# Two transposes of P in one run, and an opening whose loads wait for x

## The chip, the cores and the metric

The kernel runs on one core of one Trainium2 chip. The metric is the device time of one execution in microseconds, the median of several runs. TensorE (PE in the rows) multiplies, VectorE (DVE) and ScalarE (ACT) do the elementwise work, GpSimd (POOL) and SyncE (SP) mostly issue DMAs. An engine executes its instructions in the order in which the program lists them, and an instruction waits until what it reads is ready and what it overwrites is free.

## The reference

x has 256 rows of 1024 floats. Four layers, then one block of another kind:

```python
for i in range(DEPTH):                      # 4
    x = layer_norm(ALPHA * x + 0.5 * swiglu(x, ffn1_w13[i], ffn1_w2[i]), ...)
    y = (dsa_mixer, fox_mixer, mla_mixer)[i % 3](x, ...)
    x = layer_norm(ALPHA * x + y, ...)
    x = layer_norm(ALPHA * x + 0.5 * swiglu(x, ffn2_w13[i], ffn2_w2[i]), ...)

# the second block
qa, ka, va, u, qm, km, vm, gates = split_in(rms_norm_2(x) @ w_in)
ya = swa_attention(qa, ka, va, sinks, slopes) @ w_o_swa
z  = gelu(s5_ssm(u, ...)) @ w_glu
yb = (z[..., :512] * sigmoid(z[..., 512:])) @ w_o_ssm
yc = moba_attention(qm, km, vm, slopes) @ w_o_moba
g  = sigmoid(gates)
x  = x + (g[0] * ya + g[1] * yb + g[2] * yc) @ w_out
x  = x + square(relu(rms_norm_2(x) @ w_ff1)) @ w_ff2
```

All attention is softmax(q k^T + bias) v per head, with 16 heads in a layer's mixer and 8 + 8 in the second block. s5_ssm is a linear recurrence over the 256 rows with 32 groups of 64 complex states.

## The kernel before

All weights are streamed once, in tiles of 128 x 1024 floats that SyncE loads into five buffers named raw. A weight w is split: ScalarE rounds raw to `whi`, VectorE subtracts to get `wlo` (helpers at L242 and L250, eight buffers each), activations are split the same way, and a product is three matmuls: L417 (hi by hi), L418 (lo by hi) and L419 (hi by lo). TensorE's transposes are matmuls with the identity, at L449.

The program is written by Python generators ("threads"). Each emits the instructions of one piece of work, and `yield`s the time at which it may go on; `self.at["pe"]` is an estimated clock of TensorE, and whoever emits long streams of matmuls lets the threads that are due step in between. So the estimated times set the order in which an engine's instructions stand. At run time that order is fixed.

PSUM has eight banks: four named y, two acc and two tr. `can("tr", n)` gives the time at which n banks of that name are free. Every run of transposes takes a tr bank and gives it back when ScalarE or VectorE has copied it out.

Attention (`attend`) works in groups of up to eight heads, in two halves of even and odd heads: scores at L701 into two y banks, mask and minimum on VectorE at L713, exponential on ScalarE, sums and scaling on VectorE; then each half's P (a tile named wk) is transposed by up to four transposes, copied to SBUF (the first half by ScalarE, the second by VectorE in most stages), and multiplied with v at L758. Five stages do this: the mixers of the layers (DSA, FoX, MLA, DSA) and the second block's (SWA and MoBA).

In the second block the SSM runs beside attention, in four segments s, each a chain: eight matmuls at L1387 into two y banks; on VectorE eight products with tables named tb, two sums, eight scans (named wk) and six more operations; then

```python
            yield lambda: max(t, self.can("tr"))
            yb = self.bank("tr")
```

and output matmuls at L1428 (`part` None) and L1430 (parts 0 and 1, which read the chain's two results); a GELU on ScalarE, split into two tiles named g, which the matmuls with w_glu read. A segment's tables are loaded by GpSimd once the segment before has its output matmuls.

In the opening SyncE issues the first half of x's first 128 rows, the first weight tile in two halves and x's other parts in turn, while TensorE runs dummy matmuls (`warm`, L359) and then transposes x.

Of the kernel before, what the change touches and what calls it, by code (L numbers as in the profile page):

```python
# [17 lines left out]
P = 128  # L18
# [119 lines left out]
class Model:  # L138
# [179 lines left out]
    def setup(self):  # L318

        self.ident = self.load_const("ident", [P, P])  # L320
        self.mask = self.tile([P, S], "mask", 1)
        self.rope = self.const([P, NT, 2, 16], "rope")
        self.mh = self.const([P, 1], "mh")
        self.nc.vector.memset(self.mh, -0.5)
        self.nc.scalar.activation(self.small(1), self.mh, AF.Silu)
        x = [self.tile([P, 1024], f"x{T}", 1) for T in range(NT)]
        parts = [[(x[T][:, c:c + 512], self.ap["x"][T * P:(T + 1) * P, c:c + 512]) for c in (0, 512)] for T in range(NT)]
        self.between[0], self.between[0, 0], self.between[2] = [parts[0][0]], [parts[1][0]], [parts[0][1], parts[1][1]]
        self.between[10] = [(self.mask, self.ap["mask"]), (self.rope, self.ap["rope"])]
        self.skip = self.const([P, 8], "skip")  # L330
        self.sink = self.tile([P, 2, 8], "sink", 1)
        self.between[14] = [(self.skip, self.ap["ssm_d"]), (self.sink[:, 0], self.bcast(self.ap["sinks"], 8))]
        return x

    def opening(self, x):


        fut = [[Later() for _ in range(8)] for _ in range(2)]
        self.loads()
        self.pinned = True  # L340
        self.warm(7)
        th = [self.xT(x[T], T, fut[T], [self.at["pe"], 7400.0 + 700.0 * T], 1.0, False) for T in range(2)]
        for T in range(2):
            self.part_of(0, self.pieces[0].parts[T])
            next(th[T])
            ready = next(th[T])
            self.spawn(th[T], ready)
        self.pinned = False
        self.n_split = 1
        self.stream()  # L350
        return fut

# [11 lines left out]
    def take(self):  # L364
        p = self.pieces[self.taken]
        self.taken += 1
        return p

    def loads(self):

        while self.n_raw < len(self.plan) and self.n_raw < self.n_split + N_RAW:
            for out, src in self.between.get(self.n_raw, []):
                self.nc.sync.dma_start(out, src)
                self.at["dma"] += self.width(out) * 512 / 340.0
            ap = self.plan[self.n_raw]
            p = Piece()
            p.w = ap.shape[1]
            p.raw = self.tile([P, 1024], "raw", N_RAW)
            p.parts = [slice(c, c + 512) for c in (0, 512)] if self.n_raw < 2 else [slice(0, p.w)]
            for i, c in enumerate(p.parts):  # L380
                self.nc.sync.dma_start(p.raw[:, c], ap[:, c])
                if (self.n_raw, i) in self.between:
                    for out, src in self.between[self.n_raw, i]:
                        self.nc.sync.dma_start(out, src)
            t = max(self.at["dma"], self.pieces[self.n_raw - N_RAW].t if self.n_raw >= N_RAW else 0.0) + p.w * 512 / 340.0
            self.at["dma"] = t
            p.t_raw = t + 2200.0
            self.pieces.append(p)
            self.n_raw += 1
# [288 lines left out]
    def attend(self, T, n, q, k, v, bias, scale, o_tag, ot, o0, out, sink=None, gate=None, acts=False):  # L678
# [4 lines left out]
        W = P * (T + 1)  # L683
# [8 lines left out]
        def group(gi, grp):  # L692
            nc = self.nc
            yield lambda: INF if st["next"] < gi else max(inputs(grp), self.can("y", 2))
            sub = [[i for i in grp if i % 2 == e] for e in range(2)]
            banks = self.ybanks()
            for a in range(len(sub[0])):
                for t in range(T + 1):
                    for e in range(2):
                        i = sub[e][a]  # L700
                        nc.tensor.matmul(banks[e].v[:, a * W + t * P:a * W + (t + 1) * P], q(i).v, k(i, t).v, start=True, stop=True)  # L701
                        self.pe(218.0)
            t0 = self.pe_done()
            tiles, ready, PT = [], [], {}
            for e in range(2):
                yield lambda: self.load["act"] - self.busy
                ns = len(sub[e])
                sc, sm = self.wk([P, 512]), self.small(16)
                mx, ss, rc, sk = (sm[:, 4 * z:4 * z + ns] for z in range(4))
                for a, i in enumerate(sub[e]):  # L710
                    c = slice(a * W, (a + 1) * W)
                    bi, tb = bias(i)
                    nc.vector.tensor_tensor_reduce(out=sc[:, c], in0=banks[e].v[:, c], in1=bi, scale=-scale,  # L713
                                                   scalar=3.0e38, op0=OP.add, op1=OP.min, accum_out=mx[:, a:a + 1])
                    tm = self.run_on("dve", 70.0 + 1.04 * W, max(t0, tb))
                self.free(banks[e], tm)
                if sink is not None:
                    for a, i in enumerate(sub[e]):
                        self.V("tensor_tensor", mx[:, a:a + 1], mx[:, a:a + 1], sink(i)[0], op=OP.min)
                        tm = self.V("tensor_tensor", sk[:, a:a + 1], mx[:, a:a + 1], sink(i)[1], op=OP.add)  # L720
                for a, i in enumerate(sub[e]):
                    c = slice(a * W, (a + 1) * W)
                    tm = self.A(sc[:, c], sc[:, c], AF.Exp, bias=mx[:, a:a + 1], scale=-1.0, accum_out=ss[:, a:a + 1], after=tm)
                if sink is not None:
                    tm = self.A(sk, sk, AF.Exp, after=tm)
                    tm = self.V("tensor_tensor", ss, ss, sk, op=OP.add, after=tm)
                tm = self.V("reciprocal", rc, ss, after=tm)
                for a, i in enumerate(sub[e]):
                    c = slice(a * W, (a + 1) * W)
                    tm = self.V("tensor_scalar", sc[:, c], sc[:, c], rc[:, a:a + 1], None, op0=OP.mult, fast=True, after=tm)  # L730
                tiles.append(sc)
                ready.append(tm)
                if e == 0:
                    st["next"] = gi + 1
            for e in range(2):
                yield lambda e=e: max(ready[e], self.can("tr"))
                cols = len(sub[e]) * W
                b = self.transposes([tiles[e][:, j * P:(j + 1) * P] for j in range(cols // P)])
                pt = self.wk([P, 512])
                if e == 0 or acts:  # L740
                    t1 = self.A(pt[:, :cols], b.v[:, :cols], AF.Copy, after=self.pe_done())
                else:
                    t1 = self.V("tensor_copy", pt[:, :cols], b.v[:, :cols], after=self.pe_done())
                self.free(b, t1)
                for a, i in enumerate(sub[e]):
                    for t in range(T + 1):
                        PT[i, t] = pt[:, a * W + t * P:a * W + (t + 1) * P]
            yield lambda: max([t1, INF if st["pv"] < gi else 0.0] + [v(i, t).t for i in grp for t in range(T + 1)]
                              + [self.can(o_tag) if st["O"] is None else 0.0])
            if st["O"] is None:  # L750
                st["O"] = self.bank(o_tag)
            O = st["O"].v
            for a in range(len(sub[0])):
                for t in range(T + 1):
                    for e in range(2):
                        i = sub[e][a]
                        j = i // 2
                        nc.tensor.matmul(O[64 * e:64 * e + 64, j * P:(j + 1) * P], v(i, t).v, PT[i, t], start=t == 0, stop=t == T)  # L758
                        self.pe(self.pv)
            st["pv"] = gi + 1  # L760
            if gi == len(groups) - 1:
                m = n // 2
                hi, lo = ot
                t1 = self.split(hi[:, o0:o0 + m], lo[:, o0:o0 + m], self.tiles(O[:, :m * P]), self.pe_done())
                self.free(st["O"], t1)
                for j in range(o0, o0 + m):
                    out[j].put((hi[:, j], lo[:, j]), t1)

        for gi, grp in enumerate(groups):
            self.spawn(group(gi, grp), lambda: 0.0)  # L770
# [1107 lines left out]
```

## Time and profile before

| | |
|---|---|
| median of three runs | 2392.14 us (2390.95 to 2393.95) |
| the profiled execution: time, span | 2393.44 us, 2391.7 us |
| busy in the span: TensorE, VectorE, ScalarE, GpSimd | 99%, 71%, 54%, 3% |
| moved by DMA | 442.81 MB, 185 GB/s in the mean |

The span is the stretch of the profiled execution that the trace covers; the time beside it is what the device reports for that execution. A busy share is an average over the whole span.

### The profile page before, as it was taken

The numbers are of one execution on the slowest core, as the hardware profiler recorded it, in microseconds if no ns is written. First come the engines' busy times: TensorE is split into PE (matmuls) and PEld (weight loads), VectorE is DVE, ScalarE is ACT, GpSimd is POOL, SyncE is SP. The second block draws the span as 40 slices with busy tenths as digits, with TensorE's granted clock in tenths as the row PEclk, the third lists the DMA queues.
The fourth block names the chain that finished last, engine by engine and source line by source line (L and its number), as shares of the span: only waits on it lengthen the run. The fifth ranks groups of instructions, "written<-read, shape, count | busy, mean of one in ns | idle before, by whom it ended". The sixth has DMA issues, their size and how long they took to land. (4 is left out here: it accounts for less than half of the span.)

```text
span 2391.7 us, 35647 instructions
## 1 busy us (share of the span) xinstructions
PE 2369.9 (99%) x12999; PEld 1998.0 (84%) x12999; DVE 1703.6 (71%) x3265; ACT 1303.1 (54%) x2226; POOL 80.6 (3%) x123
## 2 busy tenths in 40 slices
PE   9999999999999999999999999999999999999998
PEld 7888888888888888888888888888878887878887
DVE  6668876576667866666778777666878777896664
ACT  6555655545547555455475555554665556845543
POOL 0000000000000000000000010000000000000000
PEclk9999999999999999999999999999999999999999
DMA  8655445555646465565454575654646665455552
GB/s 279 201 172 190 155 167 187 183 192 195 200 154 232 149 210 192 178 210 179 148 184 147 186 233 178 209 193 151 210 128 218 198 217 197 149 182 171 191 190 101
DMA packets 126481, 442.81 MB, mean 185 GB/s; under 512 B 14944, under 2 KB 17040, under 8 KB 126304
## 3 DMA queue, kind: packets, MB, share of 16 engines
q1 hardware_dynamic: 117792, 413.49, 51.9%
q0 software_dynamic: 7760, 26.05, 3.6%
q8 instruction: 102, 1.67, 0.3%
q10 hardware_dynamic: 752, 0.98, 0.1%
q14 instruction: 75, 0.61, 0.1%
HBM read 434.14 MB, written 5.80 MB: 184 GB/s over the span
## 5 line engine op out<-in xcount | busy, mean ns | idle before, releaser
L250 DVE TENSOR_TENSOR wlo<-raw,whi 128x1024 fp32r<-128x1024 f32 (+4 forms) x806 | 945.2, 1191 | 228.8 <-ACT whi L242 159.3
L242 ACT ACTIVATE whi<-raw 128x1024 fp32r<-128x1024 f32 (+4 forms) x806 | 821.0, 1031 | 299.9 <-PE ps L419 233.9
L426 PE MATMUL ps<-xt,whi 128*128 128x512 f32 x2496 | 628.9, 392 | 1.8 <-DVE h L250 1.4
L426 PEld LDWEIGHTS ps<-xt,whi 128*128 128x128 f32 x2496 | 451.8, 189 | 86.7 <-DVE h L250 3.8
L428 PEld LDWEIGHTS ps<-xt,wlo 128*128 128x128 f32 x2496 | 342.7, 190 | 25.8
L428 PE MATMUL ps<-xt,wlo 128*128 128x256 f32 x2496 | 350.7, 282 | 0.0
L417 PE MATMUL ps<-whi,g 128*128 128x512 f32 x866 | 339.2, 392 | 0.0
L418 PE MATMUL ps<-wlo,g 128*128 128x512 f32 x866 | 337.6, 390 | 0.0
L419 PE MATMUL ps<-whi,g 128*128 128x512 f32 x866 | 336.8, 389 | 0.0
L417 PE MATMUL ps<-whi,xt 128*128 128x512 f32 (+3 forms) x848 | 329.4, 389 | 2.6 <-DVE g L250 1.2
L419 PE MATMUL ps<-whi,xt 128*128 128x512 f32 (+3 forms) x848 | 320.5, 379 | 0.6 <-DVE xt L250 0.5
L418 PE MATMUL ps<-wlo,xt 128*128 128x512 f32 (+3 forms) x848 | 319.6, 377 | 0.0
L242 ACT ACTIVATE h<-ps 128x256 f32<-128x256 f32 x352 | 117.6, 377 | 352.5 <-PE ps L428 322.2
L250 DVE TENSOR_TENSOR h<-ps,h 128x256 f32<-128x256 f32 x320 | 122.4, 418 | 218.7 <-ACT h L242 217.9
L419 PEld LDWEIGHTS ps<-whi,g 128*128 128x128 f32 x866 | 162.7, 188 | 34.2 <-DVE g L250 0.2
L417 PEld LDWEIGHTS ps<-whi,g 128*128 128x128 f32 x866 | 162.9, 188 | 31.2
L418 PEld LDWEIGHTS ps<-wlo,g 128*128 128x128 f32 x866 | 163.0, 188 | 30.3
L417 PEld LDWEIGHTS ps<-whi,xt 128*128 128x128 f32 x848 | 159.7, 188 | 32.0 <-ACT xt L242 1.5
L419 PEld LDWEIGHTS ps<-whi,xt 128*128 128x128 f32 x848 | 159.4, 188 | 30.8 <-DVE xt L250 1.6
L418 PEld LDWEIGHTS ps<-wlo,xt 128*128 128x128 f32 x848 | 159.8, 188 | 25.7 <-issue 0.2
L242 ACT ACTIVATE g<-ps 128x512 f32<-128x512 f32 (+7 forms) x188 | 90.6, 495 | 94.9 <-PE ps L419 60.4
L242 ACT ACTIVATE h<-h 128x256 f32<-128x256 f32 x144 | 60.2, 418 | 134.7 <-DVE h L250 134.7
(222 smaller groups left out, 1924.7 us busy)
## 6 DMA issues: line engine op xcount, KB each, us to landing
raw<-in_f SPq DMA_DIRECT2D x526, 512.0 KB, 4.5
raw<-in_ff SPq DMA_DIRECT2D x64, 512.0 KB, 4.6
raw<-in_dsa_qkv SPq DMA_DIRECT2D x48, 512.0 KB, 5.1
raw<-in_w_in SPq DMA_DIRECT2D x40, 512.0 KB, 5.0
raw<-in_wo SPq DMA_DIRECT2D x32, 512.0 KB, 4.4
gb<-in_ln POOLq DMA_DIRECT2D x22, 512.0 KB, 4.7
raw<-in_fox_qk SPq DMA_DIRECT2D x16, 512.0 KB, 4.6
raw<-in_dsa_idx SPq DMA_DIRECT2D x16, 292.0 KB, 3.3
```

What stands on the lines that cost most here:

```text
L242: self.pin(self.nc.scalar.activation(out, in_, func, **kw))
L250: self.pin(getattr(self.nc.vector, fn)(out, *a, **kw))
L417: mm(acc, x[0], w[0], start=start, stop=False)
L418: mm(acc, x[0], w[1], start=False, stop=False)
L419: mm(acc, x[1], w[0], start=False, stop=stop)
L426: mm(acc, w, x.rearrange("p z t q->p (z t q)"), start=first, stop=False)
L428: mm(acc[:, S:], w, x[:, 0].rearrange("p t q->p (t q)"), start=False, stop=last)
```

## The change

In `attend`, the thread of a group waits until both halves are ready and two tr banks are free, and then emits the transposes of both halves one behind the other. In the opening, ScalarE's queue issues two of the loads (the first half of x's second 128 rows, and the second half of the first weight tile); on SyncE a one-element copy out of x's first half stands in front of the later loads, so that they wait until that half has landed; SyncE's first loads keep program order; six dummy matmuls in place of seven; and the first two weight tiles are split into hi and lo within the pinned part.

```diff
-        self.between[0], self.between[0, 0], self.between[2] = [parts[0][0]], [parts[1][0]], [parts[0][1], parts[1][1]]
+        self.between[0], self.between[2] = [parts[0][0]], [parts[0][1], parts[1][1]]
+        self.second_half = parts[1][0]
+        self.first_half = parts[0][0][0]
...
+        self.pinned = True
         self.loads()
-        self.pinned = True
-        self.warm(7)
+        self.warm(6)
...
+        for c in self.pieces[1].parts:
+            self.part_of(1, c)
         self.pinned = False
-        self.n_split = 1
+        self.n_split = 2
...
+    def sp_load(self, out, src):
+        ins = self.nc.sync.dma_start(out, src)
+        if self.n_raw < 16:
+            self.tc.keep_in_program_order(ins)
...
             for i, c in enumerate(p.parts):
-                self.nc.sync.dma_start(p.raw[:, c], ap[:, c])
-                if (self.n_raw, i) in self.between:
-                    for out, src in self.between[self.n_raw, i]:
-                        self.nc.sync.dma_start(out, src)
+                if (self.n_raw, i) == (0, 1):
+                    self.pin(self.nc.scalar.dma_start(*self.second_half))
+                    self.pin(self.nc.scalar.dma_start(p.raw[:, c], ap[:, c]))
+                    held = self.small(1)
+                    self.sp_load(held[0:1], self.first_half[0:1, 0:1])
+                else:
+                    self.sp_load(p.raw[:, c], ap[:, c])
...
-            for e in range(2):
-                yield lambda e=e: max(ready[e], self.can("tr"))
+            yield lambda: max(ready + [self.can("tr", 2)])
+            turned = [self.transposes([tiles[e][:, j * P:(j + 1) * P] for j in range(len(sub[e]) * W // P)]) for e in range(2)]
+            for e, b in enumerate(turned):
                 cols = len(sub[e]) * W
-                b = self.transposes([tiles[e][:, j * P:(j + 1) * P] for j in range(cols // P)])
                 pt = self.wk([P, 512])
```

The new lines shift the later ones by 15: L417 to L419 become L432 to L434, L449 L464, L701 L716, L758 L773, L1387 L1402, L1428 L1443 and L1430 L1445.

The instructions of two places, before and after. First the opening. SyncE's first loads before (x_6 and x_7 are the two row blocks of x, raw_76 is the first weight tile, raw_80 the second):

```order
L373 DMA x_6_71<-in_x 128x512
L381 DMA raw_76<-in_f 128x512
L384 DMA x_7_72<-in_x 128x512
L381 DMA raw_76<-in_f 128x512
L381 DMA raw_80<-in_f 128x512 x2
L373 DMA x_6_71<-in_x 128x512
L373 DMA x_7_72<-in_x 128x512
```

SyncE's first loads after (the second weight tile is raw_82):

```order
L377 DMA x_6_71<-in_x 128x512
L377 DMA raw_76<-in_f 128x512
L377 DMA small_80<-x_6_71 1x1
L377 DMA raw_82<-in_f 128x512 x2
L377 DMA x_6_71<-in_x 128x512
L377 DMA x_7_72<-in_x 128x512
L377 DMA raw_87<-in_f 128x1024
```

and ScalarE's first instructions after:

```order
L311 DMA ident_63<-in_ident 128x128
L325 ACT_TABLE_LOAD
L325 ACTIVATE small_69<-mh_67 128x1
L394 DMA x_7_72<-in_x 128x512
L395 DMA raw_76<-in_f 128x512
L242 ACTIVATE whi_102<-raw_76 128x512
L242 ACTIVATE xt_106<-ps_107 128x4x128
```

The third and fourth loads of SyncE moved to ScalarE, behind its table load and first activation, and the copy into small_80 took their place.

Second, TensorE in the second block's mixer, at the last of the SSM's four segments. Before, its eight input matmuls stand behind the last matmuls of an output projection (oth, otl), and the gates' matmuls (those that read xt) follow:

```order
L417 MATMUL ps_21312<-whi_21157,oth_4375_20026 128x512
L418 MATMUL ps_21312<-wlo_21158,oth_4375_20026 128x512
L419 MATMUL ps_21312<-whi_21157,otl_4376_20027 128x512
L1387 MATMUL ps_21413<-g_19834,pc_21377 128x128
L1387 MATMUL ps_21414<-g_19834,pc_21377 128x128
L1387 MATMUL ps_21413<-g_19834,pc_21377 128x128
L1387 MATMUL ps_21414<-g_19834,pc_21377 128x128
L1387 MATMUL ps_21413<-g_19834,pc_21377 128x128
L1387 MATMUL ps_21414<-g_19834,pc_21377 128x128
L1387 MATMUL ps_21413<-g_19834,pc_21377 128x128
L1387 MATMUL ps_21414<-g_19834,pc_21377 128x128
L417 MATMUL ps_21406<-whi_21221,xt_19766 128x512
```

After, seven of the eight stand behind the gates' matmuls, ahead of those with w_glu (that read g):

```order
L432 MATMUL ps_21512<-whi_21340,xt_19767 128x512
L433 MATMUL ps_21512<-wlo_21341,xt_19767 128x512
L434 MATMUL ps_21512<-whi_21340,xt_19767 128x512
L1402 MATMUL ps_21564<-g_19835,pc_21488 128x128
L1402 MATMUL ps_21563<-g_19835,pc_21488 128x128
L1402 MATMUL ps_21564<-g_19835,pc_21488 128x128
L1402 MATMUL ps_21563<-g_19835,pc_21488 128x128
L1402 MATMUL ps_21564<-g_19835,pc_21488 128x128
L1402 MATMUL ps_21563<-g_19835,pc_21488 128x128
L1402 MATMUL ps_21564<-g_19835,pc_21488 128x128
L432 MATMUL ps_21575<-whi_21399,g_21001 128x512
```

The eighth stands 102 rows earlier; between the two places are the gates' matmuls and the output of the segment before. The segment's output before (L1428, L1430), among the gates' matmuls:

```order
L417 MATMUL ps_21551<-whi_21321,xt_19766 128x512
L418 MATMUL ps_21551<-wlo_21322,xt_19766 128x512
L419 MATMUL ps_21551<-whi_21321,xt_19766 128x512
L1428 MATMUL ps_21564<-g_19834,rt_21379 32x128 x4
L1430 MATMUL ps_21564<-wk_21429,pc_21378 32x128 x4
L1430 MATMUL ps_21564<-wk_21431,pc_21378 32x128 x4
L1428 MATMUL ps_21564<-g_19834,rt_21379 32x128 x4
L1430 MATMUL ps_21564<-wk_21429,pc_21378 32x128 x4
L1430 MATMUL ps_21564<-wk_21431,pc_21378 32x128 x4
L417 MATMUL ps_21551<-whi_21333,xt_19766 128x512
L418 MATMUL ps_21551<-wlo_21334,xt_19766 128x512
```

and the first rows of it after, where L1443 and L1445 stand for L1428 and L1430:

```order
L434 MATMUL ps_21575<-whi_21411,g_21509 128x512
L1443 MATMUL ps_21615<-g_19835,rt_21490 32x128 x4
L432 MATMUL ps_21650<-whi_21423,g_21001 128x512
L433 MATMUL ps_21650<-wlo_21424,g_21001 128x512
L434 MATMUL ps_21650<-whi_21423,g_21002 128x512
L432 MATMUL ps_21650<-whi_21423,g_21001 128x512
L433 MATMUL ps_21650<-wlo_21424,g_21001 128x512
L434 MATMUL ps_21650<-whi_21423,g_21002 128x512
L432 MATMUL ps_21650<-whi_21438,g_21508 128x512
L433 MATMUL ps_21650<-wlo_21439,g_21508 128x512
L434 MATMUL ps_21650<-whi_21438,g_21509 128x512
L1445 MATMUL ps_21615<-wk_21582,pc_21489 32x128 x4
```

The output moved from among the gates' matmuls to the middle of the matmuls with w_glu.

## Rows read from the trace of the kernel before

**Rows 1.** The page's busy times: us, share of the span, instructions.

```profile
PE 2369.9 (99%) x12999; PEld 1998.0 (84%) x12999; DVE 1703.6 (71%) x3265; ACT 1303.1 (54%) x2226; POOL 80.6 (3%) x123
```

**Rows 2.** TensorE's waits, whole span: us in total, times, longest.

```profile
PE ps L417 <- ACT oth L242: 0.2, 1, 0.2
```

**Rows 3.** Windows, the second mixer: length, busy (instructions) of PE, PEld, DVE, ACT, POOL; clock, DMA.

```profile
2034.00:2162.30 128.30, 127.10 (x897) 102.08 (x896) 111.23 (x267) 79.04 (x154) 6.43 (x12) 1.00 0.51 167
```

**Rows 4.** Timeline of TensorE in the opening: start, length of the group, instructions.

```profile
1.23 3.17 PE L359 MATMUL ps<-h 128*128 128x512 bf16 x7 [1.23 <-DVE h L356]
...
8.28 1.28 PE L417 MATMUL ps<-whi,xt 128*128 128x512 f32 x2
...
9.70 0.40 PE L419 MATMUL ps<-whi,xt 128*128 128x512 f32 x1
9.93 0.40 PE L418 MATMUL ps<-wlo,xt 128*128 128x512 f32 x1
```

**Rows 5.** Timeline of ScalarE in the opening.

```profile
2.49 0.20 ACT L325 ACTIVATE small<-mh 128x1 f32<-128x1 f32 x1
...
7.60 0.63 ACT L242 ACTIVATE whi<-raw 128x512 fp32r<-128x512 f32 x1 [1.24 <-DMA raw<-in_f]
```

**Rows 6.** Timeline of SyncE's queue in the opening.

```profile
2.12 1.38 SPq L381 DMA_DIRECT2D raw<-in_f  x3
```

**Rows 7.** Timeline of TensorE around one run of transposes in layer 0's DSA.

```profile
260.57 0.39 PE L419 MATMUL ps<-whi,xt 128*128 128x512 f32 x1
260.80 0.60 PE L449 MATMUL ps<-ident,wk 128*128 128x128 f32 x4
...
261.47 0.40 PE L418 MATMUL ps<-wlo,xt 128*128 128x512 f32 x1
```

**Rows 8.** Timeline of TensorE, two runs of transposes in MLA.

```profile
1258.41 0.60 PE L449 MATMUL ps<-ident,wk 128*128 128x128 f32 x4
1259.33 0.64 PE L449 MATMUL ps<-ident,g 128*96 128x128 f32 x4 [0.32 <-ACT wk L242]
```

**Rows 9.** Timeline of TensorE at L1387 of the SSM's third segment.

```profile
2110.78 0.39 PE L419 MATMUL ps<-whi,xt 128*128 128x512 f32 x1
2111.09 1.16 PE L1387 MATMUL ps<-g,pc 64*128 64x128 f32 x16
2112.19 0.50 PE L417 MATMUL ps<-whi,xt 128*128 128x512 f32 x1
2112.53 0.39 PE L418 MATMUL ps<-wlo,xt 128*128 128x512 f32 x1
```

**Rows 10.** Timeline of VectorE: parts of the chains of the second and third segments.

```profile
2096.91 1.28 DVE L250 TENSOR_TENSOR wk<-wk,wk 128x512 f32<-128x512 f32 x2
2098.11 2.63 DVE L250 TENSOR_TENSOR_SCAN wk<-decay,wk 128x128 f32<-128x128 f32 x8
2100.66 0.68 DVE L250 TENSOR_TENSOR wk<-wk,tb 128x508 f32<-128x508 f32 x1
...
2103.07 1.22 DVE L250 TENSOR_TENSOR wlo<-raw,whi 128x1024 fp32r<-128x1024 f32 x1
...
2112.29 2.74 DVE L250 TENSOR_TENSOR wk<-ps,tb 128x256 f32<-128x256 f32 x8 [2.18 <-PE ps L1387]
2114.95 1.28 DVE L250 TENSOR_TENSOR wk<-wk,wk 128x512 f32<-128x512 f32 x2
```

**Rows 11.** Timeline of TensorE around the SSM's last segment, second mixer.

```profile
2131.77 1.16 PE L1387 MATMUL ps<-g,pc 64*128 64x128 f32 x16
2134.14 0.50 PE L417 MATMUL ps<-whi,xt 128*128 128x512 f32 x1 [1.20 <-DVE g L250]
...
2151.76 0.39 PE L419 MATMUL ps<-whi,xt 128*128 128x512 f32 x1
...
2153.53 0.50 PE L417 MATMUL ps<-whi,xt 128*128 128x512 f32 x1
```

**Rows 12.** Timeline of ScalarE at the end of that segment.

```profile
2154.08 0.44 ACT L242 ACTIVATE g<-h 128x256 fp32r<-128x256 f32 x1
```

More of the change, by code (lines that the diff above doesn't have):

```diff
@@ L372, in loads @@
             for out, src in self.between.get(self.n_raw, []):
-                self.nc.sync.dma_start(out, src)
+                self.sp_load(out, src)
                 self.at["dma"] += self.width(out) * 512 / 340.0
@@ L380, in loads @@
             for i, c in enumerate(p.parts):
-                self.nc.sync.dma_start(p.raw[:, c], ap[:, c])
-                if (self.n_raw, i) in self.between:
-                    for out, src in self.between[self.n_raw, i]:
-                        self.nc.sync.dma_start(out, src)
+                if (self.n_raw, i) == (0, 1):
[5 more added lines that the diff above has]
+                    self.sp_load(p.raw[:, c], ap[:, c])
             t = max(self.at["dma"], self.pieces[self.n_raw - N_RAW].t if self.n_raw >= N_RAW else 0.0) + p.w * 512 / 340.0
```

## The prediction

> **What bounds the kernel now.** I read the page's busy shares first: TensorE is busy 2369.9 us of the 2391.7 us span, 99% [rows 1]. So only three things can move the time: fewer or more TensorE microseconds, a wait of TensorE removed, a wait added. Next the list of TensorE's waits. Inside the five attention stages it names three: 0.2 us in FoX behind an output split on ScalarE [rows 2], 0.32 us in MLA where a run of transposes wanted a bank that ScalarE was still copying [rows 8], and 1.20 us in the second block's mixer [rows 11]. The other waits of the list are at stage borders and the opening. The windows agree: the second mixer's 128.3 us hold 127.1 us of TensorE [rows 3]. Merging P's transposes can therefore win back at most 0.2 + 0.3 + 1.2 = 1.7 us of waits. Last I read the timelines of TensorE, VectorE and ScalarE around the places where the two orders differ: the opening and the five attention stages, nothing else.
>
> **The opening.** The first half-speed matmuls (seven dummies in 3.17 us, 0.45 each) run until about 9.70, then the pitch is 0.23 [rows 4]. What arrives last is the second half of the first weight tile: SyncE issues it at 2.12 as its fourth load [rows 6], and ScalarE, idle 1.24 us for it, copies it at 7.60 [rows 5]; TensorE's matmuls on both row blocks begin at 8.28 [rows 4]. After the change ScalarE issues it behind its first activation, which ends at 2.69 [rows 5], and behind one other issue: about 3.1, 1.0 later than now. In return only four half tiles share the DMA engines instead of eight. At best the whole wait of 1.24 goes; at worst the tile lands later by the 1.0. Against it, every load behind SyncE's tiny copy now starts after x's first half has landed, so x's second halves and the second weight tile may come late. I take -0.4 us, and keep -1.2 to +1.0. The dropped dummy (0.45) is worth nothing: TensorE waits for x and the identity behind it.
>
> **The order of TensorE's work.** A run of four transposes has no price of its own: from the start of the last matmul before it at 260.57 to that of the second after it at 261.47 is 0.90 us, which is two matmuls at 0.227 and four transposes at 0.11 [rows 7]. Thirteen fewer such runs (78 before, 65 after, counted in the order lists over the five stages) save about 0.01 each, 0.1 us. The matmuls on parts of the array (scores, P.V, SSM) do have one: 0.31 from the start of the last plain matmul to theirs, 0.34 from the first plain one behind to the next, against 0.227 [rows 9], so 0.09 + 0.11 = 0.2 us per visit. Visits go from 11 to 9 in each DSA layer, 9 to 11 in FoX, 18 to 19 in MLA, 19 to 24 in the second mixer: four more in all, +0.8. Together +0.7.
>
> **Attention.** The 1.7 us of waits I count as gone. New: a pair of runs takes both "tr" banks at once, so the next transposes must wait for the copies. The nearest row is MLA's: transposes that start at 1258.41 end near 1258.9, the next ones wait 0.32 us until 1259.33 [rows 8]. The order after has five places of that distance (a pair, one or a few matmuls, then another run): two in each DSA layer, one in FoX. 5 x 0.32 = +1.6; bounds 0 and twice that. Between the pair and its P.V lie only a copy on each of ScalarE and VectorE; I price nothing there beyond this.
>
> **The SSM in the second mixer.** This is the large term. A segment of the SSM needs a "tr" bank for its output, and attention now wants two at a time, so all segments slip. Now the last segment's eight input matmuls (L1387) start at 2131.77, and from 2134.14 to 2152.0 TensorE has 78 gate matmuls, 18 us, in front of the segment's output (L1428, L1430) [rows 11]. After the change one of the eight stands early, the other seven behind all the gate matmuls, and only nine matmuls, four of L1443 (L1428 before) and nine more stand ahead of the first L1445 (L1430 before) that reads VectorE's result. TensorE reaches it in 7/8 x 1.10 (L1387's eight take 2111.09 to 2112.19 [rows 9]) + 18 x 0.227 + 0.43 for the four and their way in and out + 0.1 = 5.6 us. VectorE starts 1.20 us after the first L1387 (2111.09 [rows 9], 2112.29 [rows 10]). Its chain to the first half of the result, without the weight work between, is eight products 2.66, two sums 1.20, eight scans 2.55, four products 2.41: 8.8 us [rows 10]. Ready at 10.0, so TensorE waits 4.4. The second half needs two more operations at 0.6, against 0.2 of TensorE's: +1.0. Then the next matmul reads the GELU of this very segment: ScalarE's ends at 2154.52 [rows 12] where the next matmul started at 2153.53 [rows 11], hidden by gate matmuls now and open then: +1.0. Both accumulator banks are held by half-made sums until then; the next product wants one back after six matmuls, and ScalarE 0.44 plus VectorE 0.60 against three of those: +0.4. Sum **+6.8**. Lower bound 4.4 (the first wait alone, which the order fixes), upper 8.0 (one weight subtraction of VectorE ahead of the chain, 1.2 us as in the row at 2103.07 [rows 10]).
>
> **Sum**, on the profiled execution's 2393.44: -0.4 + 0.7 - 1.7 + 1.6 + 6.8 = +7.0, so 2400.4. That execution lies 1.3 above the median of 2392.14, within its runs' spread (2390.95 to 2393.95); from the median it is 2399.1. I say 2399.5.
>
> **Rivals.**
> *The chain is hidden (not slower).* If VectorE gets at the segment's first bank well before the last of the seven matmuls, TensorE need not stand at the last L1445, and the sum is 2392.14 - 0.4 + 0.7 - 1.7 + 1.6 = 2392.3, no change; it decides where the 10.0 us of the chain come down to TensorE's 5.6. For it: one of the eight stands early. Against: the seven fill the two banks in turn, so neither is complete before the sixth, and the order of either engine is fixed.
> *The clock falls (slower still).* No row shows TensorE idle for 4 us between matmuls. In the opening it ran at a pitch of 0.45, which is 1.2 GHz against 2.4 for 0.227, from 1.23 to 9.70 [rows 4], though the granted-clock column reads 1.00 there too. If it must climb again after the long wait, half of such a stretch is lost: 8.5/2 = 4.2, or 2.1 if the climb is half as long: 2401.6 to 2403.7. The Trainium skill, TensorE: Matmul & The Clock Gate, "Part 1: The HAM clock gate", says that an idle TensorE falls back to 1.2 GHz until it has been busy for a while; by it this case is the likelier the longer the wait, and the trace of before has nothing to check it on.
> *Faster by the opening.* The best opening, no waits for banks, waits gone and the low bound of the chain: 2392.14 - 1.2 + 0.7 - 1.7 + 4.4 = 2394.3, still not faster; only with the hidden chain does it come to 2389.9. So faster by 4.8 needs both and more.
> *The change does little.* MLA has 23 runs of transposes before and after, so there it hardly does what it says; that would leave its 0.3 us wait, nothing else.
>
> **Chances.** A measurement here tells 0.2%, 4.8 us. Forecast 0.60, of which 0.08 falls below 2396.9 (the low bound and a good opening); clock falls 0.17; hidden chain 0.19, nearly all of it within 4.8 us; faster 0.04. That is slower 0.52 + 0.17 = 0.69, same 0.08 + 0.19 = 0.27, faster 0.04. Range: 2392.5 leaves out half of the hidden chain and the faster case, some 0.14; the top is the forecast +1.4 (opening) +1.6 (banks) +1.2 (chain), 2403.7, and room for part of that with the clock case, 2406; about 0.05 lies above.
>
> **What would show it.** Right: in the second mixer a wait of TensorE for VectorE's "wk" at L1445 of 4 to 6 us after the last gate matmul, then one for ScalarE's "g" near 1 us; waits of some 0.3 us at the transposes (L464) for "wk" copies in both DSA layers; TensorE's busy time up by about 0.7; first matmuls on both blocks near 8 us instead of 8.28; the feed-forward stages unchanged. Wrong: no wait at L1445, or one under 2 us, would refute the main step; matmuls with a pitch of 0.45 behind the wait would show the clock case; long waits at L773 (P.V, L758 before) would mean that I underpriced attention itself.

## The result, and the profile after

The changed kernel takes 2413.47 us in the median of five runs (2410.97 to 2414.88), against 2392.14: ratio 1.0086, 95% interval 1.0076 to 1.0097. It is slower by some 21 us, three times what I forecast, and above my range. The page's busy times, as in [rows 1]:

```profile
PE 2380.0 (99%) x12998; PEld 2002.5 (83%) x12998; DVE 1703.2 (71%) x3265; ACT 1303.6 (54%) x2224; POOL 80.7 (3%) x123
```

VectorE and ScalarE do what they did; TensorE is 10 us longer busy with the same work, one dummy matmul less. That alone says that part of the loss is not waiting. TensorE's waits over the whole span, the first rows and a few below:

```profile
PE ps L1445 <- DVE wk L250: 6.0, 2, 5.2
PE ps L464 <- DVE g L250: 4.4, 4, 1.8
PE ps L464 <- ACT wk L242: 1.8, 1, 1.8
PE ps L432 <- ACT g L242: 1.6, 2, 1.0
...
PE ps L773 <- DVE small L728: 1.1, 1, 1.1
```

The first row is the wait at the SSM's output that I forecast, and the fourth holds the one for its GELU. The waits for ScalarE's wk and VectorE's small had no term in my sum. Those for VectorE's g are at stage borders, where before has them too.

Where a stage of the table begins and ends, TensorE's matmuls stand in the same order in both kernels, so the start of the same matmul in the two timelines tells what the stage between has cost. In the table, the first column of figures is the difference over each stage between the profiled execution of the change and that of before; the last is one of the opening-only kernel (e1, below), whose attention is unchanged, and so shows what such a difference can be without a cause.

| stage, between these times of before | forecast | change minus before | e1 minus before |
|---|---|---|---|
| opening, to 36 us | -0.4 | +0.3 | -0.3 |
| DSA, 222 to 505 | +0.2 | -1.1 | -0.3 |
| FoX, 740 to 960 | +0.5 | +5.4 | -0.3 |
| MLA, 1180 to 1510 | -0.1 | +0.2 | +0.4 |
| DSA, 1680 to 1905 | +0.2 | -1.9 | -1.3 |
| second mixer, 2010 to 2240 | +6.6 | +16.2 | +0.5 |

The forecasts are the terms of my sum by stage: visits and banks, less the waits of before in FoX (0.2), MLA (0.3) and the second mixer (1.2), and the chain's 6.8 in the last. The difference of one stage is good to little more than a microsecond: e1's profiled execution was the fastest of its ten (2392.04 against a median of 2394.43), and before's lies 1.3 above its median. Two stages carry the loss. In the second mixer, TensorE at the SSM's last segment, after:

```profile
2162.40 1.16 PE L1402 MATMUL ps<-g,pc 64*128 64x128 f32 x14
...
2168.06 0.39 PE L434 MATMUL ps<-whi,g 128*128 128x512 f32 x1
2173.68 0.65 PE L1445 MATMUL ps<-wk,pc 128*32 128x128 f32 x8 [5.24 <-DVE wk L250]
2175.13 0.66 PE L1445 MATMUL ps<-wk,pc 128*32 128x128 f32 x8 [0.79 <-DVE wk L250]
2175.56 0.65 PE L1443 MATMUL ps<-g,rt 128*32 128x128 f32 x8
2175.98 1.08 PE L1445 MATMUL ps<-wk,pc 128*32 128x128 f32 x16
2178.03 0.80 PE L432 MATMUL ps<-whi,g 128*128 128x512 f32 x1 [0.96 <-ACT g L242]
2178.62 0.63 PE L433 MATMUL ps<-wlo,g 128*128 128x512 f32 x1
...
2183.33 0.64 PE L464 MATMUL ps<-ident,g 128*128 128x128 f32 x4
```

L1445 waits 5.24 us for the chain's first result, 0.79 for its second, and the next product 0.96 for the GELU: 7.0 us, where I had 4.4 + 1.0 + 1.0 + 0.4. VectorE's timeline gives the parts:

```profile
2160.88 3.94 DVE L250 TENSOR_TENSOR wlo<-raw,whi 128x1024 fp32r<-128x1024 f32 x3
2164.74 2.73 DVE L250 TENSOR_TENSOR wk<-ps,tb 128x256 f32<-128x256 f32 x8
...
2172.95 0.68 DVE L250 TENSOR_TENSOR wk<-wk,wk 128x508 f32<-128x508 f32 x1
```

The chain starts 2.34 us after the first L1402, since a run of weight subtractions is ahead of it (I had that in my upper bound only, at 1.2 us), and ends with the first result 8.9 us later, at 2173.63; worked out from [rows 10] I had 8.8. TensorE stood at L1445 one pitch behind its last start, at some 2168.3, 5.9 after the first L1402 (I had 5.6).

What follows I had as a rival only. From 2178.03 on, the matmuls start 0.43 us apart in place of 0.23. The windows before, in and behind that stretch (the columns as in [rows 3]; the granted clock is the third figure from the end):

```profile
2160.00:2166.00 6.00, 6.00 (x42) 4.43 (x41) 5.60 (x8) 3.46 (x4) 0.00 (x0) 1.00 0.63 206
2173.70:2178.00 4.30, 2.57 (x40) 1.57 (x40) 1.34 (x2) 0.81 (x2) 0.00 (x0) 0.50 0.00 0
2178.00:2184.00 6.00, 5.97 (x17) 4.54 (x18) 1.27 (x3) 1.20 (x3) 0.00 (x0) 0.55 0.01 3
2184.00:2200.00 16.00, 16.00 (x76) 12.90 (x76) 12.61 (x16) 8.57 (x13) 0.00 (x0) 1.00 0.45 147
```

The granted clock is 1.00 before the wait, 0.50 from its end to 2178, 0.55 in the next stretch and 1.00 again from 2184 on. The first L1445 behind the wait takes 0.65 us where it takes 0.43 in the kernel e5 below, so TensorE was at 1.2 GHz by the end of the wait. From 2178.03 to 2183.33 it executes twelve matmuls in 5.30 us, where 12 x 0.227 = 2.7 would do: 2.6 lost; the three groups of L1443 and L1445 before lose another 0.9, by the same groups in e5. Together 3.5. That is one execution: the same count gives 2.4 in e2 and 2.9 in e9, two kernels below with the same wait of 5.24.

And two groups of scores are dear without any wait:

```profile
2066.88 1.16 PE L716 MATMUL ps<-g,g 64*128 64x128 f32 x8
...
2070.50 1.16 PE L716 MATMUL ps<-g,g 64*128 64x128 f32 x8
...
2072.47 1.16 PE L716 MATMUL ps<-g,g 64*128 64x128 f32 x8
...
2074.94 1.16 PE L716 MATMUL ps<-g,g 64*128 64x128 f32 x8
```

Each row is eight records, four matmuls, and takes 1.16 us. In before each run of scores in this stage has sixteen records, eight matmuls, and takes 1.16 us too:

```profile
2070.52 1.16 PE L701 MATMUL ps<-g,g 64*128 64x128 f32 x16
```

The scores of an even and an odd head read 64 rows each, in the two halves of the 128 partitions, and alternate in the program. In that order two records start within 0.01 us of each other, the next two 0.11 later. The order of the change has these four runs of one parity each, one bank's four ahead of the other's, and every record starts 0.11 behind the one before.

In FoX, TensorE waits for ScalarE's copy of P:

```profile
762.45 1.03 PE L464 MATMUL ps<-ident,wk 128*128 128x128 f32 x8
...
765.18 0.40 PE L434 MATMUL ps<-whi,xt 128*128 128x512 f32 x1
767.34 0.66 PE L464 MATMUL ps<-ident,g 128*128 128x128 f32 x4 [1.76 <-ACT wk L242]
```

The pair of runs at 762.45 holds both tr banks. The next transposes, of a tile g, stand nine matmuls behind and wait 1.76 us for ScalarE, whose timeline is:

```profile
766.20 0.51 ACT L242 ACTIVATE wk<-wk,small 128x256 f32<-128x256 f32 x1 [1.31 <-DVE small L728]
...
766.71 0.57 ACT L242 ACTIVATE wk<-ps 128x512 f32<-128x512 f32 x1
```

The copy at 766.71 stands behind an exponential that itself waits 1.31 us for VectorE. It is not slow; it is late in its queue.

The opening in the profiled execution gave back what it won:

```profile
1.19 1.28 ACT L325 ACT_TABLE_LOAD   x1 [1.19 <-PEq L1878]
1.26 0.38 ACTq L394 DMA_DIRECT2D x<-in_x  x1
1.67 0.45 ACTq L395 DMA_DIRECT2D raw<-in_f  x1
...
6.24 0.62 ACT L242 ACTIVATE whi<-raw 128x512 fp32r<-128x512 f32 x1
```

```profile
7.84 1.05 PE L432 MATMUL ps<-whi,xt 128*128 128x512 f32 x2
...
11.26 0.63 PE L464 MATMUL ps<-ident,x 128*128 128x128 f32 x4 [0.83 <-DMA x<-in_x]
```

ScalarE issues its two loads at 1.26 and 1.67, not behind its activation at 2.5 as I had it. So its copy of the tile's second half comes at 6.24 in place of 7.60 [rows 5], and TensorE's matmuls on both row blocks begin at 7.84 in place of 8.28 [rows 4]; but x's second half, now behind SyncE's copy and two more loads, makes it wait 0.83 us at 11.26. That wait is not fixed by the order: with the same opening TensorE waits for x 0.2 us in all in e9, 1.4 in e1 and 2.3 in e5.

### The profile page after: what moved, and what is told of

It is laid out like the page before. It is cut to its first block, busy times and chain, and to the rows that moved or that the text cites. A ratio compares the mean times of both kernels' runs of the same rounds, so it can differ in the third digit from the quotient of the medians.

```text
span 2410.4 us, 35623 instructions
## 1 busy us (share of the span) xinstructions
PE 2380.0 (99%) x12998; PEld 2002.5 (83%) x12998; DVE 1703.2 (71%) x3265; ACT 1303.6 (54%) x2224; POOL 80.7 (3%) x123
## 3 DMA queue, kind: packets, MB, share of 16 engines
q8 instruction: 102, 1.67, 0.3%
## 5 line engine op out<-in xcount | busy, mean ns | idle before, releaser
L432 PE MATMUL ps<-whi,g 128*128 128x512 f32 x866 | 340.5, 393 | 1.0 <-ACT g L242 1.0
L434 PE MATMUL ps<-whi,g 128*128 128x512 f32 x866 | 337.8, 390 | 0.0
L432 PE MATMUL ps<-whi,xt 128*128 128x512 f32 (+3 forms) x848 | 328.8, 388 | 1.0 <-ACT xt L242 0.6
L434 PE MATMUL ps<-whi,xt 128*128 128x512 f32 (+3 forms) x848 | 320.7, 379 | 0.5 <-DVE xt L250 0.5
L434 PEld LDWEIGHTS ps<-whi,g 128*128 128x128 f32 x866 | 163.2, 188 | 34.5 <-DVE g L250 0.2
L432 PEld LDWEIGHTS ps<-whi,g 128*128 128x128 f32 x866 | 163.4, 189 | 33.2 <-ACT g L242 1.4
L434 PEld LDWEIGHTS ps<-whi,xt 128*128 128x128 f32 x848 | 159.4, 188 | 30.7 <-DVE xt L250 1.8
L432 PEld LDWEIGHTS ps<-whi,xt 128*128 128x128 f32 x848 | 159.7, 188 | 30.3 <-ACT xt L242 1.3
```

What stands on the lines that cost most here:

```text
L432: mm(acc, x[0], w[0], start=start, stop=False)
L434: mm(acc, x[1], w[0], start=False, stop=stop)
```

## The experiments

**e1, e2, e3, e4: the parts.** Each kernel takes the opening or the attention of either side, by stage; with `attend_old` a stage keeps the loop of before, with `attend_both` that of the change (against before):

```diff
+            turned = None
+            if mode == "both":
+                yield lambda: max(ready + [self.can("tr", 2)])
...
+                if mode == "both":
+                    b = turned[e]
+                else:
+                    yield lambda e=e: max((ready if mode == "wait" else [ready[e]]) + [self.can("tr")])
+                    b = self.transposes([tiles[e][:, j * P:(j + 1) * P] for j in range(cols // P)])
```

e1, the new opening with attention as before:

> The opening of the change, attention as before. If the parts add up as the two traces' drift shows (opening +0.25 us, DSA -1.3 and -1.9, FoX +5.1, MLA +0.5, second mixer +15.5 to 16.2), this is 2392.4 us, within 0.5 of before. If instead the opening sets the loss (a late clock, loads out of step), it is 2400 or more.

e2, attention of the change with the opening of before:

> Attention of the change, opening as before. If the parts add up: 2413.2 us, all of the loss. If the opening carries part of it, less than 2408.

e3, the change without the second mixer's part:

> The whole change, but the second block's attention as before. If the loss sits in the second mixer (the SSM's last segment, the clock behind it and the extra visits): 2397.5 us, and neither a wait at the SSM's output matmuls nor slow matmuls behind it. If it is spread over the stages by the pairs themselves: above 2404.

e4, runs of eight in the two DSA layers alone:

> Only the two DSA layers transpose both halves in one run; all else as before. By the drift between the traces: -3.2 us, 2388.9. By my prediction's terms (visits -0.4, banks +0.6 in each layer): +0.4, 2392.5. If the pair costs in every stage: slower than 2394.

| | median us | ratio to before, 95% |
|---|---|---|
| e1 | 2394.43 | 1.0007 (0.9998 to 1.0016) |
| e2 | 2410.44 | 1.0075 (1.0059 to 1.0092) |
| e3 | 2396.39 | 1.0017 (1.0007 to 1.0026) |
| e4 | 2390.52 | 0.9993 (0.9984 to 1.0002) |

The opening is worth nothing that can be told from no change, and what there is leans to a loss: e1 is 2.3 us above before, the change 3.0 above e2, and the matmul at 36 us starts -0.3 to +0.7 us from where it starts in before's trace in the five kernels with the change's opening, and -1.3 to +0.2 in the seven with the old one, before among them. Attention alone carries the loss, and e3 puts 17 us of it into the second mixer; the 4 us by which e3 still lies above before are FoX's, 5.0 by the stage difference in e3. In DSA the runs of eight are no loss: e4 cannot be told from no change. By stage it has -0.9 us in the first layer, where e1, whose DSA is unchanged, has -0.3, and -1.9 in the second, where e1 has -1.3.

**e5: the clock.** Dummy matmuls a little ahead of the place where TensorE would wait, else the change:

```diff
+        z = self.ident.bitcast(BF16)
...
                 for part in (None, 0, 1):
+                    if s == 3 and k == 0 and part is None:
+                        for _ in range(44):
+                            self.pin(nc.tensor.matmul(yb.v[:, 256:], z[:, :P], z, start=True, stop=True))
```

> The whole change, plus 44 dummy matmuls (128x256, bf16, about 0.11 us each) that TensorE executes just ahead of the last SSM segment's L1443, where it would wait for VectorE anyway; they write an unused part of the bank. If the idle time is what drops TensorE's clock: the wait at L1445 shrinks from 5.2 to about 0.5, the time does not grow by the dummies' 4.8, and the matmuls behind run at a pitch of 0.23 instead of 0.43, so 2410.5, 3 us less than the change. If the slow matmuls have another cause, they stay and the time stays at 2413.5.

2409.85 us, 1.0077 (1.0063 to 1.0091): 3.6 under the change though 4.98 us of work came in. This interval and the change's overlap, so the total alone does not show it; the trace does. Its timeline of TensorE:

```profile
2166.79 4.98 PE L1442 MATMUL ps<-ident 128*128 128x256 bf16 x44
...
2174.82 0.43 PE L1449 MATMUL ps<-wk,pc 128*32 128x128 f32 x8 [0.65 <-DVE wk L250]
...
2176.26 0.43 PE L1449 MATMUL ps<-wk,pc 128*32 128x128 f32 x8 [0.59 <-DVE wk L250]
2176.50 0.40 PE L1447 MATMUL ps<-g,rt 128*32 128x128 f32 x8
2176.72 0.62 PE L1449 MATMUL ps<-wk,pc 128*32 128x128 f32 x16
2178.31 0.50 PE L432 MATMUL ps<-whi,g 128*128 128x512 f32 x1 [0.96 <-ACT g L242]
2178.65 0.40 PE L433 MATMUL ps<-wlo,g 128*128 128x512 f32 x1
2178.88 0.40 PE L434 MATMUL ps<-whi,g 128*128 128x512 f32 x1
```

and its window over the stretch behind:

```profile
2178.00:2184.00 6.00, 5.46 (x25) 4.12 (x26) 2.27 (x4) 2.83 (x6) 0.00 (x0) 1.00 0.00 0
```

The wait at the output is down to 0.65 and 0.59, GELU's 0.96 is as it was, and the clock stays at 1.00, with a pitch of 0.23. The second mixer costs 13.7 in place of 16.2 by the stage difference. So the slow matmuls come from the idle time, and cost some 2.5 to 3.5 us.

**e6: the fight for tr banks.** Before, with runs of eight in the second mixer alone, and there:

```diff
-            yield lambda: max(t, self.can("tr"))
-            yb = self.bank("tr")
+            yield lambda: max(t, self.can("y"))
+            yb = self.bank("y")
```

> Before, with runs of eight in the second block alone, and there the SSM's output takes a y bank instead of a tr bank, so that attention's pairs can't hold it up. If the fight for tr banks is what moved the last segment behind the gates: no wait at L1445, its input matmuls stand some 110 matmuls ahead of its output, and the second mixer costs 1 to 4 us (visits, waits of the pairs): 2393 to 2396. If the pairs cost by themselves: 2400 or more.

2398.23 us, 1.0027 (1.0016 to 1.0038), with no wait at the output: the second mixer costs 7.5 in place of 16.2. So the fight for tr banks is the cause of the last segment's place; e7, below, agrees. But the time does not fall to my 2393 to 2396, as another wait grew:

```profile
2136.28 0.79 PE L417 MATMUL ps<-whi,xt 128*128 128x512 f32 x1 [3.26 <-DVE g L250]
```

```profile
2136.00:2139.00 3.00, 2.72 (x6) 2.15 (x7) 3.00 (x6) 0.00 (x0) 0.08 (x1) 0.52 0.98 373
```

This is the wait of 1.20 us of [rows 11], for VectorE's gate product, grown to 3.26, and the clock falls behind it too (0.52). VectorE is late there, with three weight subtractions ahead of the gate product:

```profile
2132.13 3.49 DVE L250 TENSOR_TENSOR wlo<-raw,whi 128x1024 fp32r<-128x1024 f32 x3
2135.54 1.28 DVE L250 SCALAR_TENSOR_TENSOR g<-g,ps 128x512 f32<-128x512 f32 x2
```

Some scores still stand unpaired in this order, and it has four visits more than before.

**e7: waiting for both halves, without taking both banks.** Before, with `attend_wait` in all stages: a half's transposes wait until both halves are ready, but take one bank and stand as a run of their own.

> Before, with one half of the edit in all five stages: the transposes wait until both halves are ready, but each half then takes one tr bank and its own run of four. If taking two banks at once does the harm: FoX and the second mixer come out near before, 2392 to 2396. If waiting for both halves does it: FoX keeps its +5 and, where the order is that of the change, its waits.

2408.52 us, 1.0070 (1.0055 to 1.0085). FoX costs +5.5, as in the change, with the same wait:

```profile
771.86 0.66 PE L449 MATMUL ps<-ident,g 128*128 128x128 f32 x4 [1.77 <-ACT wk L242]
```

The order of FoX is all but that of the change. So it is the wait for both halves that costs in FoX, not the second bank. The second mixer costs 6.5, 10 less than in the change, with 0.4 us of wait at the SSM's output: there the banks make the difference. The wait for the gate product is as long as in e6, and the matmuls behind it first keep their pitch and then slow down:

```profile
2145.96 0.50 PE L417 MATMUL ps<-whi,xt 128*128 128x512 f32 x1 [3.26 <-DVE g L250]
...
2146.99 0.43 PE L418 MATMUL ps<-wlo,xt 128*128 128x512 f32 x1
2147.22 0.62 PE L419 MATMUL ps<-whi,xt 128*128 128x512 f32 x1
```

And the two DSA layers cost +3.0 and +1.2, where the runs of eight were no loss; why is not shown.

**e8: x ahead of the second weight tile.** e4 with the new opening and

```diff
-        self.between[0], self.between[2] = [parts[0][0]], [parts[0][1], parts[1][1]]
+        self.between[0], self.between[1] = [parts[0][0]], [parts[0][1], parts[1][1]]
```

> A version for best time: runs of eight in the DSA layers alone, the opening of the change, but with x's second halves loaded ahead of the second weight tile. If the parts add: DSA -1.5, opening -0.6 since TensorE need not wait 0.8 us for x at 11 us: 2390. If the second weight tile comes too late instead: a wait of 0.5 to 1.5 us of TensorE for whi or xt between 10 and 14 us, 2391 to 2392.

2390.44 us, 0.9995 (0.9987 to 1.0004): TensorE no longer waits for x's second halves; it waits 0.4 us for an earlier part of x, at 5.52, and 0.2 for a wlo. Against e4 nothing can be told.

**e9 to e12: pairs.** The scores, and in e10 to e12 P.V too, are kept in the order in which they are written:

```diff
-                        nc.tensor.matmul(banks[e].v[:, a * W + t * P:a * W + (t + 1) * P], q(i).v, k(i, t).v, start=True, stop=True)
+                        self.tc.keep_in_program_order(nc.tensor.matmul(banks[e].v[:, a * W + t * P:a * W + (t + 1) * P], q(i).v, k(i, t).v, start=True, stop=True))
```

e9, the change with this for the scores:

> The whole change, with the score matmuls kept in the order in which they are written, so that even and odd heads alternate. In the change's second mixer two groups of scores stand as four runs of four matmuls of one parity, each as long (0.89 us from first to last) as a run of eight in pairs. If pairs of 64 rows run side by side: these two groups take 0.9 us less each, one visit less, so 2 us off: 2411.4, and every run of eight scores is 16 records long. If the lone runs only look long: 2413.5 as the change.

e10, runs of eight in DSA, both kept:

> A version for best time: runs of eight in the DSA layers alone, opening as before, and scores and P.V kept in written order in all stages. Against the DSA version alone (2390.5) the order has three visits less and no lone scores in MLA: -1.0 to -1.5, so 2389 to 2389.5, 0.12% under before. If visits cost nothing here: 2390.5.

e11, e10 with the opening of e8:

> The same, with the opening of the change and x's second halves ahead of the second weight tile. If the parts add: 0 to 0.6 us under the version with the old opening. If the opening is worth nothing: the same.

e12, before with both kept:

> Before, with scores and P.V kept in written order and nothing else. If the visits and lone scores carry the gain of the two versions beside it: 2390.5 to 2391 (MLA three visits less, DSA one each). If it is the runs of eight in DSA: as before, 2392.

| | median us | ratio to before, 95% |
|---|---|---|
| e9 | 2411.19 | 1.0085 (1.0072 to 1.0099) |
| e10 | 2388.16 | 0.9989 (0.9980 to 0.9998) |
| e11 | 2389.25 | 0.9989 (0.9980 to 0.9998) |
| e12 | 2388.89 | 0.9989 (0.9980 to 0.9998) |

In e9 the second mixer costs 14.2, 2.0 less than in the change, though the waits of P.V grew by 1.0 together. Of the two groups of scores that had been split one is a full run; the other, against what I expected, stands as one matmul and seven:

```profile
2067.17 0.48 PE L716 MATMUL ps<-g,g 64*128 64x128 f32 x2
...
2070.76 1.21 PE L716 MATMUL ps<-g,g 64*128 64x128 f32 x16
...
2073.94 1.16 PE L716 MATMUL ps<-g,g 64*128 64x128 f32 x14
```

By the distances from start to start the scores of this stage take 1.7 us less than in the change. Over the whole kernel this is not to be told from the change, since FoX cost 1.7 more (7.1), with one visit more. There the clock fell behind the wait for ScalarE's copy, 1.77 us, as it did not in the change behind the same wait of 1.76; the windows behind it, first the change, then e9:

```profile
767.00:770.00 3.00, 2.66 (x13) 1.93 (x14) 3.00 (x12) 3.00 (x8) 0.54 (x1) 1.00 0.67 246
767.00:770.00 3.00, 3.00 (x12) 2.10 (x13) 3.00 (x10) 3.00 (x9) 0.27 (x1) 0.72 0.66 214
```

Seven matmuls there lose some 1.4 us.

e10 to e12 are faster than before by 0.11% each, just clear of no change, and e10 and e12 are some 1 to 2 us faster than I expected. e12 is no slower than the two that also transpose in eights, so the gain is the written order. It shows above all in MLA, where visits go from 18 to 15: in all three the time behind P.V's matmuls there is 1.4 us less, and behind the scores the same as before. The stage difference is -1.4 in e12 and -2.5 in e10 and e11; the three have the same order in MLA, so the other 1.1 is not the order's.

## Why the prediction was wrong

By the stage differences I missed 9.6 us in the second mixer (16.2 against 6.6) and 4.9 in FoX (5.4 against 0.5). The steps that failed are the clock, which my sum left out, the price of "Attention", which left out the half that waits, and the price of the visits, which left out the pairing.

**The chain.** Right in place and mechanism, and the last segment slipped for the reason given (e6). That the size comes out so near, 7.0 us against 6.8, is in part luck: the first wait was 0.8 longer than my 4.4, by the weight subtractions that I had in the upper bound only, and the 0.4 for an accumulator bank did not come.

**The clock.** I saw that the wait opens the way to it and gave it 17 in 100, at 2.1 to 4.2 us. It cost 3.5 here, and 2.4 to 2.9 in the two other executions with the same wait. The forecast should have held it: my own sum had TensorE idle for 4.4 us in one piece, and no row of before spoke for the clock surviving that. The Trainium skill, TensorE: Matmul & The Clock Gate, "Part 1: The HAM clock gate", says that an idle TensorE falls back to 1.2 GHz. The traces agree for the long waits, with a granted clock of 0.50 behind 5.24 us here and 0.52 behind 3.26 us in e6, and 1.00 where e5 left only waits of 0.65, 0.59 and 0.96. They do not tie the fall to the length of one wait alone: behind 1.76 us in FoX the clock stayed here and fell in e9.

**"Attention".** This step failed. I priced the pairs by the distance between a run and the next use of its bank (5 x 0.32) and wrote that between the pair and its P.V lie only two copies, so nothing more. The largest such wait is 1.76 us, since the copy stands behind an exponential in ScalarE's queue. One of P.V in the second mixer is 1.12; it ends with VectorE's mask and minimum (L728), which by the program reads scores out of a y bank, and P.V's output takes a y bank there, so most likely it waited for that bank. Above all I gave no price to the first half, which now waits for the second: FoX costs +5.4, and e7 shows that this edit alone does it. Of the 5.4 TensorE's waits in FoX are 1.76 + 0.32 + 0.25, less 0.2 of before: 2.1. P.V, which stood in five runs, stands in nine, three of them one matmul ahead of its seven fellows, which leaves two without a partner each time. The distances from start to start, waits taken out, put the remaining 3.3 us at 1.4 behind P.V's matmuls, 0.5 each behind the scores and the transposes, and 0.9 behind the plain matmuls between them.

**The visits.** Counted rightly (19 to 24 in the second mixer) and priced wrongly. A visit costs some 0.2, but four of the runs were scores of one parity only, and those lose the pairing: a run takes 0.89 us from its first start to its last, and two groups take it four times in place of two, +1.8; in e9 the scores take 1.7 less. One bank's name four times in a row was to be seen in the order.

**The second mixer's sum.** 7.0 (chain) + 3.5 (clock) + 1.8 (scores) + 1.1 (P.V) + 1.0 (visits) - 1.2 (the wait of before, gone) = 13.2 of the 16.2. The other 3.0 are in the timeline: 0.5 is a wait for g at 2019.25, where e1 has 0.4 too, and 2.5 lie in longer distances from start to start. Waits taken out, these add 8.8 us in this stage: 3.6 behind plain matmuls, 2.2 behind scores, 1.5 behind the SSM's output, 0.7 behind P.V, 0.5 behind transposes and 0.3 behind the SSM's input, where my terms clock, scores and visits make 6.3.

**The opening and DSA.** The opening was forecast at -0.4, and no run shows a gain. Its premise failed: the loads were issued at 1.26 and 1.67, not at 3.1, and that the matmuls on both blocks came 0.44 sooner, as I had it, is luck; that x's second halves may come late was right in this execution. DSA came out a little better than I had it, without the waits of 0.3 for banks.

## What to carry over

Waiting for the later of two inputs in order to do both at once pays only if what is merged had a price: here a run of four transposes had none, and the waiting moved everything behind it. When an order moves a dependent chain to the end of independent work, count what is left to cover it, and when that leaves an engine idle for microseconds, price the clock with it, as a range: the same wait of 5.24 us cost 2.4 to 3.5 us in three executions. Matmuls on parts of the array are to be kept in their pairs and runs: their written order alone gave 0.11% (0.02% to 0.20%), where the edit under study had at most 1.7 us of waits, 0.07%, to win.

## What the runs showed of the hardware

- A DMA on ScalarE's queue was issued at 1.26 us, 0.07 after the table load ahead of it in the program had begun; it waited neither for that (1.28 us) nor for the activation that stands between the two, which began at 2.48.
- TensorE's matmuls started 0.43 us apart in place of 0.23 behind waits of 5.24 us (the change, e2, e9) and 3.26 us (e6, e7), for six to twelve matmuls. In e7 the first five behind the wait still kept their pitch. Behind 1.77 us in FoX they slowed in e9 only; the change, e3, e5 and e7 have that wait too and keep their pitch.
- Four score matmuls of one parity take 1.16 us, as eight do that alternate between the two halves of the partitions.
